# Shifted copies of a state-space kernel matrix: by matmul, or through DRAM

## The chip, the core and the metric

The kernel runs on one core of one Trainium2 chip. The metric is the device time of one execution in microseconds (us); lower is better. The engines are named as in the profile: PE is TensorE (its matmuls; PEld is its loading of weights), DVE is VectorE, ACT is ScalarE, POOL is GpSimd, SP is the engine that issues most of the DMAs. Each engine works through its own list of instructions in order.

## The reference, cut to what matters

The model has two layers on a sequence of 256 tokens and 2048 channels. The first layer mixes tokens with a diagonal state-space model (S5), 128 groups of 16 channels with a complex state of 64 each, and then a gated linear unit (GLU) of 2048 x 4096. The second is an attention layer. Each is followed by a convolutional gated feed-forward layer.

```python
def step(carry, ub):
    h_re, h_im = carry
    x_re = jnp.einsum('blgp,gnp->blgn', ub, bb_re)
    x_im = jnp.einsum('blgp,gnp->blgn', ub, bb_im)
    ...
    acc_re, acc_im, hl_re, hl_im = lax.associative_scan(combine, (a_r, a_i, x_re, x_im), axis=1)
    hs_re = acc_re * h_re[:, None] - acc_im * h_im[:, None] + hl_re
    hs_im = acc_re * h_im[:, None] + acc_im * h_re[:, None] + hl_im
    y = (jnp.einsum('blgn,gpn->blgp', hs_re, c_re) - jnp.einsum('blgn,gpn->blgp', hs_im, c_im)
         + d_skip * ub)
    return (hs_re[:, -1], hs_im[:, -1]), y
...
y = jax.nn.gelu(y)
val, gate = jnp.split(y @ w_glu.astype(f32) + b_glu.astype(f32), 2, axis=-1)
return (val * jax.nn.sigmoid(gate)).astype(dtype)
```

Such a state-space model is linear, so its output is also a sum over earlier tokens of a small kernel matrix per group and per distance in time, times the input.

## The kernel before

The sequence is cut into 32 chunks of 8 tokens. Within a chunk the output is the input times a 128x128 block Toeplitz matrix per group (8 tokens x 16 channels on both sides): the block that leads from token s to token t depends on t - s alone. Between chunks a state is carried, by a scan on DVE.

The stage `s5` handles the 128 groups in 16 steps of 8 groups, each 2 columns `g` (NG) by 4 rows `j` of groups. For one step n:

- `lead` / `part_a` builds, on DVE, `f1`, `f2` and `e1` (the powers of the state's decay with C and B multiplied in) from loads `bc` and `g4`. `powers` runs every fourth step, `frames` (sines and cosines) every second.
- `part_k` turns the input to `U` and computes with 16 small matmuls the kernel matrix `K`: 32 rows for each `j`, of which the upper 16 are used, and for each `g` 240 columns, 128 of kernel values and 112 of zeros. Then the Toeplitz matrix `TP` is made from it: its row block s is the row block of `K` shifted by 16 s columns. ACT evicts `K` from PSUM, and DVE adds the skip term to it (L452).
- `part_e` transposes `e1` to `ET`. `part_v` gives the chunk's contribution to the state `vs`, `part_r` turns and scans it to `R`, `part_h` gives the states `H` before each chunk.
- `part_c` adds the local part (`U` with `TP`) and the carried part (`H` with `f1`, `f2`) to the output `py`, which goes through a GELU to `yg`. `part_d` transposes four steps' worth of `yg` to the GLU's input.
- After every fourth step four units of early GLU work come free (`glu_early`, 24 matmuls of 128x512 on a 1 MB piece of weights each); one is taken per step.

The loop is software-pipelined: iteration n does `part_v` and `part_r` of step n-1, `part_c` of step n-2, `part_k` and `part_e` of step n, and `lead` of step n+1. A scheduling layer then fixes the order on each engine; the code's order and its dependencies are its input, and it may take instructions of neighbouring steps past each other.

`T` makes a buffer: `K` has 2 (`Ks`), `TP` 2, `U` 3. PSUM has 8 banks, 4 under the name `wk` and 4 under `acc`. The early GLU units use two `acc` banks each.

All small matmuls go through `tiled`, which uses a quarter of PE's columns at a time: 32 columns, with `tile_position` going through 0, 32, 64, 96 in turn.

Of the kernel before, what the change touches and what calls it, by code (L numbers as in the profile page):

```python
# [8 lines left out]
F32 = mybir.dt.float32  # L9
F32R = mybir.dt.float32r  # L10
I32 = mybir.dt.int32
AF = mybir.ActivationFunctionType
# [3 lines left out]
P = 128  # L16
# [21 lines left out]
HOLD = ((0, 2), (4, 6), (8, None), (None, None))  # L38

C_ID, C_PS, C_PR, C_BO, C_DM, C_MK, C_CV = 0, 128, 256, 384, 512, 528, 592  # L40
C_SG, C_NSG, C_TPI, C_FR, C_RS, C_HP, C_MH, C_END = 624, 625, 626, 627, 628, 629, 630, 638


@with_exitstack
def tile_trunk(ctx: ExitStack, tc: tile.TileContext, a: dict):
    nc = tc.nc
    act, dve, pool, pe, sync = nc.scalar, nc.vector, nc.gpsimd, nc.tensor, nc.sync
    cnt = [0]

    def T(pl, shape, dt=F32, tag=None, bufs=None):  # L50
        cnt[0] += 1
        kw = {"bufs": bufs} if bufs else {}
        return pl.tile(shape, dt, tag=tag, name=f"{tag}_{cnt[0]}", **kw)
# [8 lines left out]
    def wk():  # L62
        return T(ps, [P, 512], F32, "wk")
# [4 lines left out]
    cst = T(cp, [P, C_END], F32, "cst")  # L68
# [190 lines left out]


    def s5(f):
        with tc.tile_pool(name="s5", bufs=2) as q1, tc.tile_pool(name="s5d", bufs=4, space=bass.MemoryType.DRAM) as dp:
            w0 = env["wp"]
            dt = T(q1, [P, P], F32, "dt", 1)
            sync.dma_start(dt, a["sL"].partition_broadcast(P))
# [28 lines left out]
            r, nn = T(q1, [P, P], F32, "R"), T(q1, [P, P], F32, "w2")  # L294
# [94 lines left out]
            NG = 2  # L389
# [4 lines left out]
            def tiled(*terms):  # L394
                o = wk()[:, : NG * P]
                for g in range(NG):
                    for i, (lhs, rhs) in enumerate(terms):
                        for j in range(4):
                            pe.matmul(  # L399
                                o[32 * j : 32 * j + 32, g * P : (g + 1) * P], lhs(g, j), rhs(g, j),  # L400
                                start=g == 0 and i == 0, stop=g == NG - 1 and i == len(terms) - 1,
                                tile_position=(0, 32 * j),
                            )
                return o

            def by_group(z):
                return z.rearrange("p (g t) -> p g t", g=NG)

            def flat2(z):
                return z.rearrange("p s q -> p (s q)")  # L410
# [27 lines left out]
            def part_k(sb, e1, ff):  # L438
                puv = wk()[:, : NG * P].rearrange("p (g t) -> p g t", g=NG)
                for g in range(NG):  # L440
                    gi = NG * sb % 8 + g
                    pe.transpose(puv[:, g, :], Xn[sb // PB][:, gi, :], ident)
                U = T(q1, [P, NG, P], F32, "U", 3)
                act.activation(U, puv, AF.Copy)

                def e67(g, j):
                    return flat2(e1[:, 4 * g + j, 6:8, :])

                pkg = by_group(tiled(*((e67, lambda g, j, z=z: flat2(z[:, 4 * g + j, 1:9, :])) for z in ff)))
                K = Ks[sb % 2]  # L450
                act.activation(K[:, :, :112], pkg[:, :, :112], AF.Copy)
                dve.tensor_tensor(  # L452
                    K[:, :, 112:128],
                    pkg[:, :, 112:128],
                    dB.rearrange("p (g q) -> p g q", q=16)[:, NG * sb : NG * (sb + 1), :],
                    op=ALU.add,
                )
                RW = 4 * NG * 240
                kd = T(dp, [32, RW], F32, "kd")
                act.dma_start(kd.rearrange("r (j w) -> j r w", j=4), K.rearrange("p g c -> p (g c)"))  # L460
                TP = T(q1, [P, 4, NG, 240], F32, "TP")
                TPf = TP.rearrange("p j g c -> p (j g c)")[:, : RW - 112]
                act.dma_start(TPf, bass.AP(kd.tensor, kd.offset + 16 * RW, [[16, 8], [RW, 16], [1, RW - 112]]))
                return U, TP

            def part_e(e1):
# [47 lines left out]

            def part_c(sb, yg, ff, U, TP, H):
                def h(g, j):
                    return H[:, 4 * g + j, :]

                py = tiled(
                    (lambda g, j: U[:, g, 32 * j : 32 * j + 32], lambda g, j: TP[:, j, g, :P]),  # L520
                    *((h, lambda g, j, z=z: flat2(z[:, 4 * g + j, 0:8, :])) for z in ff),
                )
                o = (sb % PB) * 16 * NG
                act.activation(
                    yg[:, :, o : o + 16 * NG].rearrange("p t (g q) -> p g t q", q=16),
                    py.rearrange("p (g t q) -> p g t q", g=NG, q=16),
                    AF.Gelu_apprx_tanh,
                )
# [19 lines left out]

            todo, ab, fr, U, TP, ET, H = [], {}, {}, {}, {}, {}, {}
            nb = 4 * PB  # L550
# [16 lines left out]
            for n in range(nb + 2):  # L567
                if 0 <= n - 1 < nb:
                    vs = part_v(U[n - 1], ET.pop(n - 1))
                if n >= 2:  # L570
                    m = n - 2
                    if m % PB == 0:
                        yg = T(q1, [P, 8, P], F32, "yg", 1)
                    part_c(m, yg, ab.pop(m)[1], U.pop(m), TP.pop(m), H.pop(m))
                if 0 <= n - 1 < nb:
                    R = part_r(n - 1, vs, *fr[n - 1])
                if n < nb:
                    U[n], TP[n] = part_k(n, *ab[n])
                    ET[n] = part_e(ab[n][0])
                if 0 <= n - 1 < nb:  # L580
                    H[n - 1] = part_h(n - 1, R, *fr.pop(n - 1))
                if n >= 2 and m % PB == PB - 1:
                    part_d(m // PB, yg)
                    todo.append(glu_steps(m // PB))
                lead(n + 1)
                if n < 3:
                    scale_x(rs, n + 1)
                if todo and next(todo[0], True) is True:
                    todo.pop(0)
# [453 lines left out]
    ng = a["norm_g"]  # L1043
    f = f_pair()
    todo = s5(f)
    env["ap"] = ctx.enter_context(tc.tile_pool(name="ap", bufs=1))
    env["xp"] = ctx.enter_context(tc.tile_pool(name="xp", bufs=1))
# [28 lines left out]
def _constants():  # L1076
    import numpy as np

    c = np.zeros((P, C_END), np.float32)
    p = np.arange(P)  # L1080
    c[p, C_ID + p] = 1.0
    c[p, C_PS + (p + 64) % P] = 1.0
    c[p, C_PR + (p ^ 32)] = 1.0
    c[:, C_BO : C_BO + P] = (p[:, None] % 32) == (p[None, :] % 32)
    c[:, C_DM : C_DM + 16] = (p[:, None] % 32 - 16) == np.arange(16)[None, :]
    c[:64, C_MK : C_MK + 64] = -1e30
    c[:, C_CV : C_CV + 32] = np.arange(32)
    sg = np.where(p < 64, -1.0, 1.0)
    c[:, C_SG] = sg
    c[:, C_NSG] = -sg  # L1090
    c[:, C_TPI] = -sg * TWO_PI
    fr = np.float32(10000.0) ** (-np.arange(0, 64, 2, dtype=np.float32) / np.float32(64))
    c[:, C_FR] = fr[p % 32]
    c[:, C_RS] = np.where(p % 64 < 32, -1.0, 1.0)
    c[:, C_HP] = math.pi / 2
    c[:, C_MH : C_MH + 8] = -0.5
    return c


def _arrays(i):  # L1100
# [8 lines left out]
    def blocks(re, im):  # L1109
# [4 lines left out]
    pn = lambda v: v.reshape(KT, P).T  # L1114
    arrays = {
        "cst": _constants(),
        "x": g("x")[0],
        "xs": g("x")[0].reshape(32, 8, 4, 512).transpose(1, 2, 0, 3).reshape(8, P, 512),
# [46 lines left out]
```

## Time and profile before

| what | value |
|---|---|
| median of 3 runs | 2263.45 us (2258.99 to 2265.07) |
| the profiled execution | 2263.12 us, span 2261.3 us |
| busy, share of the span: PE | 2087.9 us, 92% |
| DVE | 1412.9 us, 62% |
| ACT | 1095.6 us, 48% |
| POOL | 76.5 us, 3% |
| DMA, mean over the span | 174 GB/s |

The busy shares are means over stages of different kinds. The 16 steps of the state-space model lie between 20 and 312 us; the rest of the GLU, the feed-forward layers and the attention layer follow, with PE busy nearly all of the time. The profile's rows are read so: a line of the kernel, the engine, the operation, the buffer written and those read, then how many, and how long. An entry such as `[8.14 <-DMA TP<-kd]` says that the engine was idle for 8.14 us before the row, and that the transfer into `TP` ended that. PEclk is the clock that PE was granted, as a share of full speed. A line of a helper such as `tiled` (L399) stands for many uses; the names tell them apart (`wk<-TP,U`, `wk<-f,H`, `wk<-f,e`, `wk<-ET,U`).

### The profile page before, as it was taken

Reading aid. Unit: us, or ns where it says so; the run is one execution under the profiler, and the core shown is the slowest. Engines: PE = TensorE matmul, PEld = TensorE weight load, DVE = VectorE, ACT = ScalarE, POOL = GpSimd, SP = SyncE. Lnnn points to the kernel's source line nnn. Section 1 sums busy time; section 2 is a strip of 40 time slices with the busy share of each in tenths; the row PEclk is TensorE's granted clock in tenths of the full one; section 3 lists DMA queues with packets and bytes.
Section 4 is the critical chain, followed back from the end, with each engine's and each line's share of the span. In section 5 each row is a group of like instructions: output and inputs, shape, how many; then the busy total and the mean of one; then the engine's idle time right before and its main releaser. Section 6 shows DMA issues by size and latency. Waiting matters only on the chain. (4 is left out here: it accounts for less than half of the span.)

```text
span 2261.3 us, 30415 instructions
## 1 busy us (share of the span) xinstructions
PE 2087.9 (92%) x12244; PEld 1769.7 (78%) x12244; DVE 1412.9 (62%) x1904; ACT 1095.6 (48%) x1655; POOL 76.5 (3%) x93
## 2 busy tenths in 40 slices
PE   2576789899999999999998999989999999999997
PEld 1455567688888888888886899878888888888886
DVE  6777756666546655665667666476645655665566
ACT  5454434445545544553454455545545543554444
POOL 0000001200000000000002000120000000000001
PEclk9788899999999999999999999999999999999999
DMA  4455577646555555555555433545555555565554
GB/s 147 108 130 120 131 210 220 184 152 199 184 194 187 186 186 192 188 180 194 193 191 166 135 117 122 189 166 164 185 186 192 186 186 190 190 197 185 189 186 149
DMA packets 285245, 393.28 MB, mean 174 GB/s; under 512 B 9392, under 2 KB 198448, under 8 KB 284080
## 3 DMA queue, kind: packets, MB, share of 16 engines
q1 hardware_dynamic: 280816, 372.60, 50.8%
q10 hardware_dynamic: 4288, 18.74, 3.6%
q8 instruction: 96, 1.57, 0.3%
q14 instruction: 45, 0.37, 0.1%
HBM read 385.29 MB, written 6.03 MB: 173 GB/s over the span
## 5 line engine op out<-in xcount | busy, mean ns | idle before, releaser
L74 DVE TENSOR_TENSOR wlo<-raw,whi 128x1024 fp32r<-128x1024 f32 (+2 forms) x640 | 763.8, 1196 | 590.2 <-ACT whi L73 586.9
L73 ACT ACTIVATE whi<-raw 128x1024 fp32r<-128x1024 f32 (+2 forms) x640 | 658.0, 1031 | 646.5 <-PE wk L114 233.8
L114 PE MATMUL wk<-act,whi 128*128 128x512 f32 x2688 | 944.9, 396 | 0.0
L115 PE MATMUL wk<-act,wlo 128*128 128x256 f32 x2688 | 754.4, 281 | 0.0
L114 PEld LDWEIGHTS wk<-act,whi 128*128 128x128 f32 x2688 | 504.3, 188 | 121.0
L115 PEld LDWEIGHTS wk<-act,wlo 128*128 128x128 f32 x2688 | 507.9, 189 | 0.3
L109 PE MATMUL acc<-wlo,hh 128*128 128x512 f32 x652 | 255.8, 392 | 0.5
L108 PE MATMUL acc<-whi,hh 128*128 128x512 f32 x652 | 255.5, 392 | 0.0
L110 PE MATMUL acc<-whi,hl 128*128 128x512 f32 x652 | 254.4, 392 | 0.0
L109 PEld LDWEIGHTS acc<-wlo,hh 128*128 128x128 f32 x652 | 122.5, 188 | 28.5 <-DVE wlo L74 2.2
L108 PEld LDWEIGHTS acc<-whi,hh 128*128 128x128 f32 x652 | 122.5, 188 | 27.3 <-ACT hh L73 0.5
L110 PEld LDWEIGHTS acc<-whi,hl 128*128 128x128 f32 x652 | 122.5, 188 | 26.9
L109 PE MATMUL acc<-wlo,act 128*128 128x512 f32 (+1 forms) x332 | 129.6, 392 | 4.3 <-DVE wlo L74 4.2
L108 PE MATMUL acc<-whi,act 128*128 128x512 f32 (+1 forms) x332 | 130.0, 395 | 0.8 <-ACT act L73 0.4
L110 PE MATMUL acc<-whi,act 128*128 128x512 f32 (+1 forms) x332 | 127.3, 385 | 0.0
L166 POOL TENSOR_TENSOR f<-f,gb 128x512 f32<-128x512 f32 x24 | 38.1, 1593 | 1901.5 <-issue 1586.3
L109 PEld LDWEIGHTS acc<-wlo,act 128*128 128x128 f32 x332 | 65.0, 196 | 20.1 <-DVE wlo L74 8.2
L755 DVE SCALAR_TENSOR_TENSOR cv<-gs,cw,cv 128x255 f32<-128x255 f32 (+1 forms) x168 | 77.1, 480 | 3.0
L108 PEld LDWEIGHTS acc<-whi,act 128*128 128x128 f32 x332 | 64.7, 197 | 14.9 <-ACT whi L73 1.7
L110 PEld LDWEIGHTS acc<-whi,act 128*128 128x128 f32 x332 | 64.5, 194 | 11.3 <-issue 0.2
L753 ACT ACTIVATE cv<-gs,cb,cw 128x256 f32<-128x256 f32 x84 | 50.4, 601 | 36.7 <-DVE gs L705 36.7
L399 PE MATMUL wk<-TP,U 128*32 128x128 f32 x256 | 20.5, 369 | 47.4 <-DMA TP<-kd 42.5
(281 smaller groups left out, 2377.7 us busy)
## 6 DMA issues: line engine op xcount, KB each, us to landing
raw<-in_w_gate SPq DMA_DIRECT2D x88, 1024.0 KB
raw<-in_w_up SPq DMA_DIRECT2D x88, 1024.0 KB
raw<-in_w_down SPq DMA_DIRECT2D x88, 1024.0 KB
raw<-in_w_glu SPq DMA_DIRECT2D x32, 1024.0 KB
raw<-in_w_o SPq DMA_DIRECT2D x16, 1024.0 KB
TP<-kd ACTq DMA_DIRECT2D x16, 904.0 KB
raw<-in_w_ukv SPq DMA_DIRECT2D x8, 1024.0 KB
gb<-in_norm_g SPq DMA_DIRECT2D x6, 1024.0 KB
```

The costliest lines, as they stand in the source:

```text
L73: act.activation(hi, src, AF.Copy)
L74: (eng or dve).tensor_tensor(lo, src, hi.bitcast(F32), op=ALU.subtract)
L108: pe.matmul(o, lh, rh, start=first, stop=False)
L109: pe.matmul(o, lh, rl, start=False, stop=False)
L110: pe.matmul(o, ll, rh, start=False, stop=last)
L114: pe.matmul(ov, lh, r, start=first, stop=False)
L115: pe.matmul(ov[:, 0, :], ll, r[:, 0, :], start=False, stop=last)
L166: (dve if n == NCH - 1 else pool).tensor_tensor(c, c, g[0][:, n * 512 : (n + 1) * 512], op=ALU.mult)
L399: pe.matmul(o[32 * j : 32 * j + 32, g * P : (g + 1) * P], lhs(g, j), rhs(g, j), start=g == 0 and i == 0, stop=g == NG - 1 and i == len(ter ...
L753: act.activation(cv[:, ft, :], gv[:, ft, :], AF.Identity, scale=cw[:, 2, n : n + 1], bias=cb[:, n : n + 1])
L755: dve.scalar_tensor_tensor(cv[:, ft, sh:], gv[:, ft, : S - sh], cw[:, 2 - sh, n : n + 1], cv[:, ft, sh:], op0=ALU.mult, op1=ALU.add,)
```

## The change

Before, `part_k` wrote `K` to a DRAM buffer `kd` with one DMA, laid out as 32 rows, and read it back with a second DMA whose address pattern starts each of 8 row blocks 16 columns further on. Both DMAs were issued from ACT's queue, and the second waits for the first.

After, `TP` is made by matmuls. For each `j` and each shift, a 128x32 selection matrix of zeros and ones (a slice of the constant table, which grows from 638 to 894 columns) picks the 16 rows of `K` that belong to `j` and puts them into 16 of 32 output rows, while the moving operand is `K` from column r on, 128 columns for each of the two `g`. An even and an odd shift share 32 output rows and are added up in PSUM. That makes 2 x 2 x 2 x 4 = 32 matmuls a step into two `acc` banks, and ACT evicts each bank with one copy of 128x512. `TP` loses the zero padding: 128 instead of 240 columns per group.

```diff
-C_SG, C_NSG, C_TPI, C_FR, C_RS, C_HP, C_MH, C_END = 624, 625, 626, 627, 628, 629, 630, 638
+C_SG, C_NSG, C_TPI, C_FR, C_RS, C_HP, C_MH, C_SL, C_END = 624, 625, 626, 627, 628, 629, 630, 638, 894
...
-                RW = 4 * NG * 240
-                kd = T(dp, [32, RW], F32, "kd")
-                act.dma_start(kd.rearrange("r (j w) -> j r w", j=4), K.rearrange("p g c -> p (g c)"))
-                TP = T(q1, [P, 4, NG, 240], F32, "TP")
-                TPf = TP.rearrange("p j g c -> p (j g c)")[:, : RW - 112]
-                act.dma_start(TPf, bass.AP(kd.tensor, kd.offset + 16 * RW, [[16, 8], [RW, 16], [1, RW - 112]]))
+                TP = T(q1, [P, 4, NG * P], F32, "TP")
+                for jj in range(2):
+                    bank = accb()
+                    for j in range(2):
+                        for odd in range(2):
+                            o = C_SL + (2 * (2 * jj + j) + odd) * 32
+                            for b in range(4):
+                                r = 16 * (2 * b + odd)
+                                pe.matmul(
+                                    bank[32 * b : 32 * b + 32, j * 256 : (j + 1) * 256].rearrange("p (g c) -> p g c", g=NG),
+                                    cst[:, o : o + 32], K[:, :, r : r + P],
+                                    start=j == 0 and odd == 0, stop=j == 1 and odd == 1, tile_position=(0, 32 * b),
+                                )
+                    act.activation(TP[:, 2 * jj : 2 * jj + 2, :], bank.rearrange("p (j c) -> p j c", j=2), AF.Copy)
                 return U, TP
...
-                    (lambda g, j: U[:, g, 32 * j : 32 * j + 32], lambda g, j: TP[:, j, g, :P]),
+                    (lambda g, j: U[:, g, 32 * j : 32 * j + 32], lambda g, j: TP[:, j, g * P : (g + 1) * P]),
...
+    for j in range(4):
+        for odd in range(2):
+            q = np.arange(16)
+            c[32 * j + 16 + q, C_SL + (2 * j + odd) * 32 + 16 * odd + q] = 1.0
```

The lines behind the change are 8 higher than before (L503 becomes L511), and the new matmuls are L466, the new evictions L471. What this does to the order is shown at two places. The first is PE's list in the step n = 2, before the change: the transposes of `e`, the matmul on `R` of the step before, then `ET,U` (for `vs`) mixed with the first matmuls on `TP` of the step before.

```order
L471 MATMUL wk_519<-cst_73,e_108_417 128x128 x4
L471 MATMUL wk_525<-cst_73,e_108_417 128x128 x4
L503 MATMUL wk_531<-R_488,cst_73 128x256
L399 MATMUL wk_563<-ET_518,U_493 32x128 x4
L399 MATMUL wk_575<-TP_383,U_360 32x128
L399 MATMUL wk_563<-ET_518,U_493 32x128 x4
L399 MATMUL wk_575<-TP_383,U_360 32x128 x3
```

The same place on PE after the change:

```order
L479 MATMUL wk_616<-cst_73,e_110_481 128x128 x4
L479 MATMUL wk_622<-cst_73,e_110_481 128x128 x4
L466 MATMUL acc_579<-K_43_178,cst_73 32x256 x16
L466 MATMUL acc_597<-K_43_178,cst_73 32x256 x16
L511 MATMUL wk_628<-R_552,cst_73 128x256
L399 MATMUL wk_660<-ET_615,U_557 32x128 x8
L399 MATMUL wk_672<-TP_412,U_391 32x128 x4
```

The 32 new matmuls stand between the transposes of `e` and the matmul on `R`, and need `K` of the same step; everything behind them is in the old order.

The second place is ACT's list one step earlier, before the change: the eviction of `K`, those of `ET`, the store of `K`, `vs`, other work, and then the load of `TP`, ahead of the next output (L524).

```order
L451 ACTIVATE K_44_181<-wk_362 128x2x112
L472 ACTIVATE ET_385<-wk_386 128x512
L472 ACTIVATE ET_385<-wk_392 128x512
L460 DMA kd_381<-K_44_181 4x32x480
L478 ACTIVATE vs_447<-wk_438 128x2x128
L479 ACTIVATE vs_447<-wk_438 128x2x64
L420 ACTIVATE bc_538<-bc_538,cst_73 128x128
L421 ACTIVATE bc_538<-bc_538 128x128
L494 ACTIVATE dc_45_184<-mag_18_114 128x8x31
L73 ACTIVATE whi_975<-raw_969 128x1024
L463 DMA TP_383<-kd_381 128x1x1808
L524 ACT_TABLE_LOAD
```

And after it:

```order
L451 ACTIVATE K_44_179<-wk_393 128x2x112
L480 ACTIVATE ET_449<-wk_450 128x512
L480 ACTIVATE ET_449<-wk_456 128x512
L420 ACTIVATE bc_815<-bc_815,cst_73 128x128
L502 ACTIVATE dc_45_182<-mag_18_112 128x8x31
L419 ACTIVATE bc_635<-bc_635,cst_73 128x128
L421 ACTIVATE bc_815<-bc_815 128x128
L471 ACTIVATE TP_412<-acc_413 128x512
L471 ACTIVATE TP_412<-acc_431 128x512
L486 ACTIVATE vs_511<-wk_502 128x2x128
L487 ACTIVATE vs_511<-wk_502 128x2x64
```

The two DMAs are gone, and two evictions of `TP` stand ahead of the two of `vs`.

More of the change, by code (lines that the diff above doesn't have):

```diff
@@ L261, in s5 @@
     def s5(f):
-        with tc.tile_pool(name="s5", bufs=2) as q1, tc.tile_pool(name="s5d", bufs=4, space=bass.MemoryType.DRAM) as dp:
+        with tc.tile_pool(name="s5", bufs=2) as q1:
             w0 = env["wp"]
```

## Prediction

> **What bounds the kernel now.** I read the busy time by stretch first, then the waits in the stretch that the change touches, then the instructions in order of time. The end of the program is set by TensorE (PE), and from 312 us on the order of its instructions is the same in both programs but for a few neighbours. So the question is how long the state-space stage lasts, from 20 us to 312 us. Columns after the stretch: busy us of PE, PEld, DVE, ACT, POOL with instruction counts, then the granted PE clock, the DMA share and GB/s.
>
> ```profile
> 54.90:119.80 64.90, 41.60 (x556) 32.11 (x557) 48.91 (x85) 26.85 (x64) 0.18 (x2) 0.73 0.43 107
> ...
> 20.00:312.00 292.00, 188.93 (x2058) 142.90 (x2062) 210.24 (x339) 130.12 (x282) 1.35 (x6) 0.81 0.52 127
> ```
>
> PE works 189 of 292 us, at a granted clock of 0.81; DVE works 210. No engine is full, so the stage is a chain with holes. These are the holes between 20 and 320 us (us in total, times, longest):
>
> ```profile
> PE wk L399 <- DMA TP<-kd: 42.5, 12, 8.6
> PE wk L399 <- ACT ET L472: 15.2, 6, 7.1
> ...
> ACT vs L478 <- PE wk L399: 23.3, 8, 7.4
> ACT vs L478 <- DMA kd<-K: 22.6, 4, 9.3
> ACT bc L420 <- DMA bc<-in_sBC: 22.2, 4, 9.8
> ...
> ACT act L73 <- DMA kd<-K: 12.7, 3, 5.5
> ACT L524 <- DMA kd<-K: 9.6, 1, 9.6
> ...
> DVE w L490 <- PE wk L488: 39.3, 8, 9.0
> ```
>
> PE stands 42.5 us before the matmuls that need `TP`. ACT stands another 44.9 us (22.6, 12.7 and 9.6) before the issue of the load, because its queue is in order and the load waits for the store. DVE's largest hole, 39.3 us, is PE's hole passed on. One round trip shows why:
>
> ```profile
> 44.89 0.55 ACTq L460 DMA_DIRECT2D kd<-K  x1
> 57.60 0.61 ACTq L463 DMA_DIRECT2D TP<-kd  x1
> 70.05 0.39 PE L399 MATMUL wk<-TP,U 128*32 128x128 f32 x1 [8.14 <-DMA TP<-kd]
> ```
>
> The store is issued at 44.9, the load can be issued at 57.6, the matmul starts at 70.1: 25 us for one step, two in flight.
>
> **Removed.** (1) The PE waits for `TP`: -42.5. DVE was idle 81.8 us of the 292, more than all that is removed, so I take the whole; if DVE is late next, half of it. (2) ACT's stand before the load. PE felt it where `vs` was queued behind it:
>
> ```profile
> 132.57 0.47 PE L487 MATMUL wk<-cst,vs 128*128 128x128 f32 x1 [4.77 <-ACT vs L478]
> 151.03 0.47 PE L487 MATMUL wk<-cst,vs 128*128 128x128 f32 x1 [3.11 <-ACT vs L478]
> 299.34 0.47 PE L487 MATMUL wk<-cst,vs 128*128 128x128 f32 x1 [3.89 <-ACT vs L478]
> ```
>
> Together -11.8. The rest of ACT's 44.9 lies beside PE's own waits and is not counted again.
>
> **Added on PE.** Each of the 16 steps gets 32 fp32 matmuls, 32 columns wide, 256 elements moving, four column groups in turn. The nearest rows are the same form with 128 moving, at a low and at a full clock (each fp32 matmul is two records, so x8 is four matmuls):
>
> ```profile
> 85.39 0.68 PE L399 MATMUL wk<-TP,U 128*32 128x128 f32 x8
> 85.81 1.11 PE L399 MATMUL wk<-f,H 128*32 128x128 f32 x16
> ...
> 126.97 0.40 PE L399 MATMUL wk<-TP,U 128*32 128x128 f32 x8
> 127.19 0.62 PE L399 MATMUL wk<-f,H 128*32 128x128 f32 x16
> ```
>
> Start to start, four matmuls take 0.42 us slow and 0.22 us fast: 105 and 55 ns each. With 256 elements 210 and 110 ns, so 32 take 6.72 or 3.52 us a step, and 16 steps 107.5 or 56.3 us. That is the largest term, and its size hangs on the clock. Cheaper than 56.3 it can't be, since the fast row is already at full clock.
>
> The clock moves the old work too. In a step 24 matmuls stand on `TP` and `H` (24 x 50 ns = 1.2 us between slow and fast), six transposes of `vs` and `U`, and 16 matmuls on `f` and `e`:
>
> ```profile
> 87.12 0.42 PE L488 MATMUL wk<-cst,vs 128*128 128x128 f32 x1
> 87.33 0.42 PE L487 MATMUL wk<-cst,vs 128*128 128x128 f32 x1
> 88.33 1.68 PE L399 MATMUL wk<-f,e 128*32 128x128 f32 x32
> ...
> 116.97 1.08 PE L399 MATMUL wk<-f,e 128*32 128x128 f32 x32
> 117.98 0.77 PE L471 MATMUL wk<-cst,e 128*128 128x128 f32 x5
> ...
> 140.12 0.27 PE L488 MATMUL wk<-cst,vs 128*128 128x128 f32 x1
> 140.22 0.27 PE L487 MATMUL wk<-cst,vs 128*128 128x128 f32 x1
> ```
>
> A transpose is 0.21 or 0.10 us (six: 0.64), the `f,e` group 1.68 or 1.08 us (0.60). Together 2.44 us a step, 39 us in the stage, to be had at most. Call h the share of work at half speed (granted clock = 1 - h/2). New work less what the old work gains is then 56.3 + 51.2 h - 39 (1 - h) = 17.3 + 90 h us, between 17.3 and 107.3. Where PE has few holes the clock is this:
>
> ```profile
> 300.00:320.00 20.00, 18.60 (x118) 14.61 (x117) 12.96 (x20) 7.62 (x10) 0.00 (x0) 0.88 0.57 166
> 380.00:400.00 20.00, 20.00 (x90) 16.27 (x88) 11.75 (x13) 9.45 (x10) 0.00 (x0) 1.00 0.70 200
> ```
>
> 0.88 and 1.00, near 0.95, so h = 0.1: +26.3. I take it because the 8 us holes go and 3.5 us of solid work come in.
>
> **New waits.** PE now needs `K` itself, right behind the transposes of `e`. Before, only a DMA waited for it, so the trace has the time at which it was ready: the end of DVE's L452, against PE's next matmul there (L503), which would now be the first of the 32.
>
> ```profile
> 77.22 0.60 PE L503 MATMUL wk<-R,cst 128*128 128x256 f32 x2
> 77.08 0.18 DVE L452 TENSOR_TENSOR K<-wk,dB 128x32 f32<-128x32 f32 x1
> 91.35 0.70 PE L503 MATMUL wk<-R,cst 128*128 128x256 f32 x2 [0.32 <-DVE R L498]
> 92.82 0.19 DVE L452 TENSOR_TENSOR K<-wk,dB 128x32 f32<-128x32 f32 x1 [0.28 <-ACT K L451]
> 104.67 0.61 PE L503 MATMUL wk<-R,cst 128*128 128x256 f32 x2
> 105.63 0.18 DVE L452 TENSOR_TENSOR K<-wk,dB 128x32 f32<-128x32 f32 x1
> 255.41 0.60 PE L503 MATMUL wk<-R,cst 128*128 128x256 f32 x2
> 255.57 0.18 DVE L452 TENSOR_TENSOR K<-wk,dB 128x32 f32<-128x32 f32 x1
> ```
>
> `K` came 0.04, 1.66, 1.14 and 0.34 us late, 0.80 in the mean: 16 x 0.80 = +12.7, ends 0 and 26.6 (always 1.66). Behind it wait the `R` matmul, the next step's `vs` and DVE's scan.
>
> ACT gets 32 evictions of 128x512. The same form is this:
>
> ```profile
> L472 ACT ACTIVATE ET<-wk 128x512 f32<-128x512 f32 x32 | 18.1, 594 | 4.1 <-PE wk L471 2.0 <-DVE w L505 1.0 <-DVE w L506 0.4
> ```
>
> 32 x 0.594 = 19.0 us. ACT works 130 of 292, and nobody needs `TP` for a step; but the second eviction stands ahead of `vs` in ACT's queue. PE meanwhile does the `R` and `ET,U` matmuls, some 0.35 us at full clock, so about 0.25 us shows: +4, ends 0 and 19.0.
>
> PE changes between full and column-group matmuls twice more a step. After the fast `f,e` group (16 x 55 ns = 0.88) the next row begins 1.01 us later: 0.13 us a change, 32 changes, +4.2; ends 0 and, at the 0.18 us by which a fast group outlasts its next start, 5.8.
>
> **DMA.** Between 40 and 320 us these two queues move nearly all (MB, share of the 16 engines' time), and ACT's, q10, has nothing but these stores and loads:
>
> ```profile
> q10 hardware_dynamic: 4284, 18.74, 28.8%
> q1 hardware_dynamic: 9611, 16.94, 23.6%
> ```
>
> Without q10 the `bc` and weight loads land sooner. PE felt those through `ET` (15.2 us); half of it, -7, ends -15.2 and 0. The ACT queue loses 32 issues; SP's queue changes order a little and loses none. The constant table grows by 128 x 256 x 4 = 131 KB; at 127 GB/s +1.0 ahead of the inputs.
>
> **The sum.** -42.5 - 11.8 + 26.3 + 12.7 + 4.0 + 4.2 - 7.0 + 1.0 = -13.1. The profiled execution took 2263.12 us, 0.3 under the median of the runs, so 2250.0.
>
> **The rivals.** *All covered:* PE stays at full clock (h = 0), `K` is ready in time and the evictions are hidden. For it: 16 steps without a hole over 2 us. Against: DVE would then work 210 of some 253 us, in order. -54.3 + 17.3 + 4.2 - 7 + 1 = -38.8, 2224. With h = 0 alone and the rest as summed, 17.3 stands for 26.3, and the time is 2241; it belongs to this case, a quarter of its chance. The Trainium skill's page TensorE: Matmul & The Clock Gate, section "Why this matters for your kernels", asks only that no idle gap exceeds about 3 us, which would make h = 0 wherever such holes go. The trace agrees from 380 to 400 us (1.00), and not from 300 to 320 us (0.88).
>
> *The evictions show:* all 19.0 us of ACT's new work end up on the path, behind the second bank and ahead of `vs`, and 2250 + 15 = 2265: no change. For it: ACT's waits on PE for `vs` (23.3 us) show that this edge is tight. Against: the first of the two banks is free while PE works on the second. The Trainium skill's page TensorEngine Tiling (Array Packing), section "Performance Considerations", warns of just this: tiling speeds up the matmuls and not the emptying of PSUM, which may become the bottleneck. No run so far shows it here.
>
> *PE turns the bound at half clock:* the 32 matmuls stand behind the wait for `K`; if that hole and the wait for `vs` keep the clock at 0.75 (h = 0.5; the first steps had 0.73), 17.3 + 45 takes the place of 26.3: +36, 2286, slower. It decides from h = 0.25, a granted clock of 0.88, on. Against: those steps had 8 us holes.
>
> **How the numbers follow.** My forecast 0.42, all covered 0.16, no change (evictions, or h near 0.25) 0.22, half clock 0.20. A measurement of this kernel tells about 0.3% (6.8 us) from no change, so faster 0.58, same 0.22, slower 0.20. The range reaches from 2222, just under the rival with all covered, to 2284, just short of half clock.
>
> **What would show it.** No wait on `TP`; the 32 matmuls at 3.5 to 4 us a step; granted clock in the stage near 0.95; PE's waits on `K` near 13 us; ACT's 32 new evictions near 0.6 us; `bc` waits shorter; the last `TP` matmul some 13 us earlier. Wrong it is if the clock stays at 0.8, if the 32 matmuls don't run four abreast, or if DVE takes over the holes.

## The result and the profile after

The changed kernel took 2209.59 us (median of four runs, 2207.51 to 2211.37), the kernel before in the same session 2262.15 us. The ratio is 0.9759, 95% interval 0.9731 to 0.9786: 2.4% faster, some 54 us where 13 were forecast, and below the forecast range. The profiled execution has a span of 2207.7 us.

From the second half of the GLU on, the two profiles differ by a nearly constant shift. A landmark there is line 191 (PE), whose first and last starts stand behind the durations (ns, least, median, most). First before, then after:

```profile
L191 PE MATMUL acc<-xh,f x128: 270/275/552, 456.2 to 1521.6; 128*128 128x128 f32 x128
```

```profile
L191 PE MATMUL acc<-xh,f x128: 270/275/553, 405.3 to 1468.3; 128*128 128x128 f32 x128
```

50.9 us are won ahead of that line's first start, and 53.3 by its last. The stretches that were shown of before now read so (same columns):

```profile
20.00:312.00 292.00, 255.16 (x3265) 185.56 (x3266) 248.86 (x381) 182.68 (x354) 7.80 (x11) 0.98 0.35 107
...
20.00:263.00 243.00, 210.73 (x3064) 151.14 (x3068) 210.70 (x337) 158.87 (x322) 1.32 (x6) 0.98 0.25 73
...
54.90:119.80 64.90, 56.80 (x911) 39.09 (x901) 63.74 (x109) 40.82 (x89) 0.40 (x5) 0.97 0.21 60
```

The granted clock rose from 0.81 to 0.98, the DMA share fell from 0.52 to 0.35. The stage now ends at 263 us, and up to there PE and DVE both work 211 of 243 us; from 54.9 to 119.8 us DVE is busy 63.7 of 64.9. The stage is no longer a chain with holes: in that stretch DVE is nearly full, and PE not far from it. The waits between 20 and 320 us:

```profile
PE wk L495 <- ACT vs L486: 7.7, 5, 4.2
...
PE acc L466 <- DVE K L452: 4.7, 7, 1.1
...
ACT whi L73 <- DMA raw<-in_w_glu: 14.4, 6, 3.8
ACT TP L471 <- PE acc L466: 10.9, 12, 1.6
ACT bc L420 <- DMA bc<-in_sBC: 8.0, 7, 1.9
...
DVE w L498 <- PE wk L496: 4.3, 3, 2.2
```

PE waits neither for `TP` nor for `ET` any more. The wait that was put in, PE for `K`, is 4.7 us in all. ACT's waits for `bc` fell from 22.2 to 8.0, DVE's hole of 39.3 to 4.3. The new matmuls, in order of time on PE:

```profile
58.67 1.09 PE L479 MATMUL wk<-cst,e 128*128 128x128 f32 x8
60.17 3.66 PE L466 MATMUL acc<-K,cst 128*32 128x256 f32 x64 [0.41 <-DVE K L452]
63.77 0.70 PE L511 MATMUL wk<-R,cst 128*128 128x256 f32 x2
```

32 of them (64 records) take 3.60 us from start to start, 112 ns each; 16 steps make 57.6 us. The last of the rows answering to those before are ACT's evictions and, from the DMA table between 40 and 320 us, the only queue left besides instruction fetch:

```profile
L471 ACT ACTIVATE TP<-acc x32: 573/582/599, 41.9 to 247.2; 128x512 f32<-128x512 f32 x32
```

```profile
q1 hardware_dynamic: 15024, 29.60, 34.8%
```

### The profile page after: what moved, and what is told of

It reads as the page before. It is cut to its first block, busy times and chain, and to the rows that moved or that the text cites. A ratio compares the mean times of both kernels' runs of the same rounds, so it can differ in the third digit from the quotient of the medians.

```text
span 2207.7 us, 32426 instructions
## 1 busy us (share of the span) xinstructions
PE 2109.7 (96%) x13268; PEld 1779.4 (81%) x13268; DVE 1415.1 (64%) x1904; ACT 1125.0 (51%) x1695; POOL 75.7 (3%) x93
## 5 line engine op out<-in xcount | busy, mean ns | idle before, releaser
L108 PE MATMUL acc<-whi,hh 128*128 128x512 f32 x652 | 255.6, 392 | 0.0
L108 PEld LDWEIGHTS acc<-whi,hh 128*128 128x128 f32 x652 | 122.5, 188 | 27.4 <-ACT hh L73 0.5
L108 PE MATMUL acc<-whi,act 128*128 128x512 f32 (+1 forms) x332 | 126.4, 381 | 0.9 <-ACT act L73 0.7
L109 PE MATMUL acc<-wlo,act 128*128 128x512 f32 (+1 forms) x332 | 124.8, 377 | 2.3 <-DVE wlo L74 2.3
L110 PE MATMUL acc<-whi,act 128*128 128x512 f32 (+1 forms) x332 | 124.2, 375 | 0.0
L166 POOL TENSOR_TENSOR f<-f,gb 128x512 f32<-128x512 f32 x24 | 37.3, 1555 | 1866.7 <-issue 1583.9
L108 PEld LDWEIGHTS acc<-whi,act 128*128 128x128 f32 x332 | 62.5, 188 | 12.7 <-ACT act L73 1.0
L466 PE MATMUL acc<-K,cst 128*32 128x256 f32 x1024 | 60.3, 388 | 5.0 <-DVE K L452 4.7
```

Of the source, the lines that this page charges most:

```text
L108: pe.matmul(o, lh, rh, start=first, stop=False)
L109: pe.matmul(o, lh, rl, start=False, stop=False)
L110: pe.matmul(o, ll, rh, start=False, stop=last)
L166: (dve if n == NCH - 1 else pool).tensor_tensor(c, c, g[0][:, n * 512 : (n + 1) * 512], op=ALU.mult)
L466: pe.matmul(bank[32 * b : 32 * b + 32, j * 256 : (j + 1) * 256].rearrange("p (g c) -> p g c", g=NG), cst[:, o : o + 32], K[:, :, r : r + P ...
```

## The experiments

The question is why 54 us came and not 13. Each kernel ran beside the kernel before on the same chip, so kernels are compared by their ratio to it; one hundredth of a ratio is 22.6 us. The scheduler orders some instructions of e1, e2, e4 and e7 otherwise than in the kernel that they start from; what that is worth was not measured.

| kernel | median us | ratio to before, 95% interval |
|---|---|---|
| after | 2209.6 | 0.9759 (0.9731 to 0.9786) |
| e1 before, DMAs issued by POOL | 2247.9 | 0.9931 (0.9910 to 0.9952) |
| e2 before, with the new matmuls unread | 2248.1 | 0.9939 (0.9920 to 0.9957) |
| e3 after, with store and load unread | 2248.3 | 0.9940 (0.9921 to 0.9960) |
| e4 after, new matmuls twice | 2258.2 | 0.9988 (0.9976 to 0.9999) |
| e5 after, ungated load unread | 2301.0 | 1.0167 (1.0138 to 1.0196) |
| e6 as e3, four `bc` | 2238.8 | 0.9892 (0.9867 to 0.9917) |
| e7 before, four `bc` | 2259.0 | 0.9987 (0.9970 to 1.0003) |
| e8 after, four `bc` | 2205.8 | 0.9745 (0.9721 to 0.9770) |
| e9 after, constant `TP` | 2188.4 | 0.9693 (0.9676 to 0.9709) |
| e10 as e9, with store and load unread | 2239.8 | 0.9908 (0.9876 to 0.9939) |
| e11 after, with the store unread | 2233.0 | 0.9887 (0.9873 to 0.9902) |
| e12 as e8, `f2` on POOL | 2237.5 | 0.9910 (0.9896 to 0.9925) |
| e13 as e11, four `bc` | 2212.0 | 0.9765 (0.9744 to 0.9786) |
| e14 after, gated load unread | 2247.3 | 0.9918 (0.9889 to 0.9948) |
| e15 as e8, skip term on PE | 2205.4 | 0.9743 (0.9720 to 0.9766) |
| e16 after, landing tile for `bc` | 2208.6 | 0.9751 (0.9724 to 0.9778) |
| e17 as e16, with store and load unread | 2219.2 | 0.9797 (0.9769 to 0.9825) |
| e18 as e16, skip term on PE | 2210.2 | 0.9758 (0.9733 to 0.9784) |

### The parts of the change: e1 to e4

e1 is the kernel before with its two DMAs issued from POOL's queue, so that ACT no longer stands before the load:

```diff
-                act.dma_start(kd.rearrange("r (j w) -> j r w", j=4), K.rearrange("p g c -> p (g c)"))
+                pool.dma_start(kd.rearrange("r (j w) -> j r w", j=4), K.rearrange("p g c -> p (g c)"))
...
-                act.dma_start(TPf, bass.AP(kd.tensor, kd.offset + 16 * RW, [[16, 8], [RW, 16], [1, RW - 112]]))
+                pool.dma_start(TPf, bass.AP(kd.tensor, kd.offset + 16 * RW, [[16, 8], [RW, 16], [1, RW - 112]]))
```

> The kernel before, with its store of K and its load of TP issued from POOL's queue, so that ACT never stands before the load; the round trip itself stays. Theory (the length of the round trip holds PE): PE still waits 30 us or more for TP, the time falls by no more than 12 us, about 2250 to 2262. Rival (ACT's standing in line was the cost): ACT's waits on the store were 50 us in all, and with them gone at least half of the gain of the change appears, 2235 or less.

It won 15.6 us (0.0069), which lies between the two ranges and nearer the theory. PE's wait for the round trip stayed as it was (PE's waits, 20 to 312 us):

```profile
PE wk L399 <- DMA TP<-kd: 40.8, 11, 10.6
```

So ACT's stand before the load seems to have a price of its own, near the 11.8 of the forecast, and it isn't the missing 40 us.

e2 is the kernel before with the 32 selecting matmuls put in behind the load; nobody reads their result, and they aren't evicted:

```diff
+                for jj in range(2):
+                    bank = accb()
+                    ...
+                                pe.matmul(
...
```

> The kernel before with the 32 selecting matmuls of each step added, their banks left unread, while TP still comes through DRAM. Theory (the wait decides, a warm clock alone buys nothing): some 57 us of new PE work, part of it in the holes; PE still waits 25 us or more for TP, granted clock up from 0.81 to 0.88 or more, time 2260 to 2290. Rival (the gain is PE's clock, and the matmuls bring it by filling the holes): clock near 1.0 and the time 2245 or less.

With 57 us more work on PE the kernel before became 13.8 us faster, not slower, so the theory is out; the rival's 2245 us and a clock near 1.0 were not quite reached either. PE's waits in e2:

```profile
PE wk L499 <- ACT vs L490: 28.6, 9, 5.2
...
PE wk L399 <- DMA TP<-kd: 3.8, 3, 2.3
```

The matmuls went into the holes before `TP` (42.5 us before, 3.8 now), and the granted clock of the stage rose from 0.81 to 0.93, with which the old work grew shorter (PE was busy for 20.5 us with the matmuls on `TP` before, and for 13.8 in e2). What PE waits for instead is ACT's `vs`. So with the wait for `TP` nearly gone and the new matmuls done, only 13.8 of the 54 us are there.

e3 is the kernel after with the removed store and load put back into a tile that nobody reads:

```diff
+                RW = 4 * NG * 240
+                kd = T(dp, [32, RW], F32, "kd")
+                pool.dma_start(kd.rearrange("r (j w) -> j r w", j=4), K.rearrange("p g c -> p (g c)"))
+                TQ = T(q1, [P, 4, NG, 240], F32, "TQ", 1)
+                TQf = TQ.rearrange("p j g c -> p (j g c)")[:, : RW - 112]
+                pool.dma_start(TQf, bass.AP(kd.tensor, kd.offset + 16 * RW, [[16, 8], [RW, 16], [1, RW - 112]]))
```

> The changed kernel with the store and the load still done, into a buffer that nobody reads, from POOL's queue, so that only the traffic of 18.7 MB comes back. Theory (PE's waits behind late bc and weight loads came from that traffic, some 16 us): 2217 to 2230, ACT's waits on bc and on weights up by 10 us or more. Rival (traffic costs nothing, all of the gain is the wait for TP): 2207 to 2213.

It lost 40.9 of the 54.5 us (0.0181), far more than the theory's range allows. All other instructions of PE, DVE, ACT and SP are the same in the same order, so this is the price of 16 stores and 16 loads that no other work needs. The waits of ACT, DVE and PE show who pays:

```profile
ACT bc L420 <- DMA bc<-in_sBC: 36.9, 9, 8.4
...
DVE bc L418 <- DMA bc<-in_sBC: 31.6, 7, 7.9
...
PE wk L501 <- ACT vs L492: 29.4, 7, 8.9
```

And one load of `bc`, from SP's issue to ACT's first use of it, first in the kernel after:

```profile
62.06 0.33 SPq L415 DMA_DIRECT2D bc<-in_sBC  x1
...
64.67 0.40 ACT L420 ACTIVATE bc<-bc,cst 128x128 f32<-128x128 f32 x1 [0.17 <-DMA bc<-in_sBC]
```

and then the same load in e3:

```profile
59.61 0.33 SPq L415 DMA_DIRECT2D bc<-in_sBC  x1
...
70.48 0.40 ACT L420 ACTIVATE bc<-bc,cst 128x128 f32<-128x128 f32 x1 [8.43 <-DMA bc<-in_sBC]
71.28 0.36 ACT L492 ACTIVATE vs<-wk 128x256 f32<-128x256 f32 x1
```

2.6 us after the issue in the one, 10.9 us in the other, and `vs`, for which PE waits, stands right behind it in ACT's queue. Over the loads of `bc` from 20 to 312 us the time from issue to landing (least, median, most) is, after and in e3:

```profile
DMA to landing us min/median/max: 2.5/2.6/6.8
```

```profile
DMA to landing us min/median/max: 2.5/6.6/10.8
```

One thing differs from the kernel before: e3 sends the traffic out from POOL's queue (q0, 7424 packets between 20 and 312 us), the kernel before from ACT's (q10, 4288). e2 still has it on ACT's, and there too `bc` lands late:

```profile
DMA to landing us min/median/max: 6.5/7.3/11.8
```

e2 stands 40.7 us (0.0180) above the kernel after, as e3 does. But ACT's waits for the store (16.0 and 8.7 us), PE's 3.8 us for `TP` and another order are in that difference as well, so the price of the traffic on ACT's queue alone is not measured.

e4 makes every selecting matmul of the kernel after twice:

```diff
-                    for j in range(2):
+                    for rj in range(4):
+                        j = rj % 2
```

> The changed kernel with every selecting matmul done twice, 64 a step, the second set starting the sums anew. Theory (PE is now the fuller engine, with 32 us of holes left in the stage, half of which can't be filled): 57 us more PE work, time up by 30 to 55 us, 2240 to 2265. Rival (DVE sets the pace, with 211 of 243 us, and PE's work lies beside it): up by less than 20 us, under 2230.

The second dose cost 51.8 us (0.0229) for its 57.6 us of work: it finds hardly any holes. Stage and DVE's longest wait in e4:

```profile
20.00:312.00 292.00, 264.52 (x4111) 183.79 (x4112) 215.73 (x339) 151.89 (x315) 1.30 (x6) 1.00 0.21 61
```

```profile
DVE w L515 <- PE wk L512: 31.5, 13, 7.6
```

PE at 264.5 of 292 us and at full clock is then the bound. The kernel after stands just short of that.

### Traffic and matmuls apart: e9 and e10

In e9 the matmuls and evictions of the kernel after are replaced by one constant tile; e10 adds the unread store and load of e3.

```diff
-                TP = T(q1, [P, 4, NG * P], F32, "TP")
-                for jj in range(2):
-                    ...
+                if "TPc" not in env:
+                    env["TPc"] = T(q1, [P, 4, NG * P], F32, "TPc", 1)
+                    pool.memset(env["TPc"], 0.0)
+                TP = env["TPc"]
```

> The kernel after without the selecting matmuls and their evictions; TP is one constant tile, so the shift is left out, and there is neither matmul nor DRAM traffic nor a wait for TP. It prices the first dose of the 57.7 us of selecting matmuls, as e4 priced the second (+48.6 us). If PE bounds the stage of the kernel after already: 2155 to 2175 us. If VectorE, busy 39 of 40 us there between 60 and 140 us, stands ready as the next bound: 2180 to 2200 us, with VectorE busy over 92% of the stage and the first matmuls nearly free. If the matmuls were wholly covered: 2203 to 2210 us.

> As e9, with the store and load of K put back from POOL's queue into a tile that nobody reads: traffic without the matmuls and without the wait for TP. Contention theory: the loads of bc land in 6 to 7 us in place of 2.6, and ACT and VectorE stand behind them as in e3, whether or not there are matmuls: 2225 to 2248 us, close to e3's 2248 and 35 us or more above e9. Rival (in e3 the traffic only slowed PE's own work, the matmuls and the transfers together): within 15 us of e9.

| ratio to before | no matmuls | matmuls | matmuls cost |
|---|---|---|---|
| no traffic | e9 0.9693 | after 0.9759 | 0.0066, 14.9 us |
| traffic | e10 0.9908 | e3 0.9940 | 0.0032, 7.2 us |
| traffic costs | 0.0215, 48.6 us | 0.0181, 40.9 us | |

Both came as the contention theory, and DVE as the next bound, had it. The traffic costs 41 to 49 us whether or not PE makes the shift, and the matmuls 7 to 15 us of their 57.6. The middle of the stage shows why; the stretch 60 to 200 us in e9, after and e3:

```profile
60.00:200.00 140.00, 107.86 (x1316) 79.77 (x1308) 134.94 (x222) 83.19 (x170) 0.22 (x3) 0.94 0.28 76
```

```profile
60.00:200.00 140.00, 126.58 (x1878) 90.32 (x1879) 130.36 (x209) 97.11 (x190) 0.40 (x5) 0.99 0.25 70
```

```profile
60.00:200.00 140.00, 109.10 (x1551) 77.51 (x1544) 108.29 (x175) 78.89 (x157) 10.59 (x18) 0.90 0.58 130
```

Without matmuls DVE is busy 134.9 of 140 us: DVE is nearly the floor, and most of the work of PE's matmuls lies beside it. In e9 PE waits for DVE:

```profile
PE wk L399 <- DVE e L435: 32.5, 9, 7.7
```

After, DVE works 130.4 and PE 126.6 of 140. With the traffic neither reaches 110. (The scheduler orders some instructions of e9 and e10 otherwise than those of after and e3; each pair that gives the price of traffic has one order.)

### Which transfer, and through which wait: e5, e11, e14, e6, e7, e8, e13

e5 was to give the load without the store: `K` is stored once, and the load repeated in every step. Against e3:

```diff
-                kd = T(dp, [32, RW], F32, "kd")
-                pool.dma_start(kd.rearrange("r (j w) -> j r w", j=4), K.rearrange("p g c -> p (g c)"))
+                if "kd" not in env:
+                    env["kd"] = T(dp, [32, RW], F32, "kd", 1)
+                    pool.dma_start(env["kd"].rearrange("r (j w) -> j r w", j=4), K.rearrange("p g c -> p (g c)"))
+                kd = env["kd"]
```

> The kernel after, with the load of 128 x 1808 words from DRAM put back in every step from POOL's queue into a tile that nobody reads; the store of K is made once, in the first step, so that after it no transfer hangs on K and K's buffer is held by none. Contention theory (the bytes of the round trip hold up the other queue's loads of bc, ACT and VectorE stand, PE stands behind them): the load has about 926 KB of the 1,170 KB of store and load, so most of the 39 us that store and load together cost the kernel after comes back: 2232 to 2250 us, ACT's waits for bc 25 us or more in 20 to 312 us. Rival (the 39 us came from the wait of the store for K, from K's buffer held by the store, or from the order): 2208 to 2220 us, waits for bc near the 8 us of the kernel after.

2301 us, outside both ranges and inconclusive. Held by no store, each load followed as soon as the one before had landed, and two small fills of `z` stood behind them in POOL's queue, for which DVE waited:

```profile
DVE pu L370 <- POOL z L358: 70.8, 1, 70.8
```

e14 mends that with a store of 16 columns (8 KB) ahead of each load, which ties it to its step; e11 has the store and no load.

```diff
+                pool.dma_start(kd.rearrange("r (j w) -> j r w", j=4)[:, :, 112:128], K[:, 0, 112:128])
```

> The kernel after with, in each step from POOL's queue, a store of 16 columns of K (8 KB) and behind it the whole load of 904 KB, read by nobody: the load's bytes at nearly e3's moments, without the store's. If the bytes set the price: 2232 to 2245 us. If the store, being issued just ahead of the loads of bc, has most of e3's 39 us, and the load falls between them: 2212 to 2228 us. POOL's two small fills of z stand behind these transfers in its queue, so up to 20 us could come from there; VectorE's waits for z would show it.

> The kernel after with the store of K alone (240 KB a step from POOL's queue), read by nobody. If the bytes set the price, a fifth of the 39 us of e3 at most: 2210 to 2222 us, loads of bc landing in about 3 us. If the store's wait for K, its hold on K's buffer or the issue from POOL's queue set it: 2230 to 2250 us.

The load, with its small store, costs 36.0 us over the kernel after (0.0159), and DVE does not wait for the fills of `z` there; the store alone, with a fifth of the bytes, 29.0 (0.0128); together they cost 40.9. So the bytes don't set the price, and for the store the theory that they do falls. In e11 the median landing of `bc` grows by 1.1 us only, to 3.7, yet ACT stands 20 us longer:

```profile
ACT bc L420 <- DMA bc<-in_sBC: 28.4, 8, 5.7
```

In most steps of e11 the store of `K` is issued within two us of a load of `bc`, in some before it and in some behind. The rows of the same load show one before it:

```profile
60.48 0.69 POOL L474 DMA_DIRECT2D kd<-K  x1 [10.58 <-DVE K L452]
...
62.01 0.33 SPq L415 DMA_DIRECT2D bc<-in_sBC  x1
...
68.42 0.40 ACT L420 ACTIVATE bc<-bc,cst 128x128 f32<-128x128 f32 x1 [3.96 <-DMA bc<-in_sBC]
```

Issued 1.5 us behind the store, the load is used 6.4 us later, where it took 2.6 in the kernel after. e13 takes the coincidence away with four buffers for `bc`; e8, e7 and e6 have the same edit in the kernel after, in the kernel before and in e3:

```diff
-                bc4 = T(q1, [P, 4, NP, 16], F32, "bc")
+                bc4 = T(q1, [P, 4, NP, 16], F32, "bc", 4)
```

> e11 (the kernel after with the store of K beside it, 2233 us) with four buffers for bc. If the store costs its 23 us only because it is issued within two us of a load of bc that ACT soon waits for, then loads issued one or two steps ahead hide the longer landing: 2205 to 2217 us, ACT's waits for bc under 10 us (28.4 in e11). If the store's bytes or its hold on K's buffer slow the stage in another way: 2225 to 2236 us.

> The kernel after with four buffers for bc. ACT still waited 8 us for bc there (7 waits). If these are on the path: 2200 to 2207 us. If PE, which is busy 211 of 243 us there, covers them: 2207 to 2213 us. A changed order of the loads could also cost some us.

> The kernel before with four buffers for bc in place of two and nothing else. If late loads of bc were a loss of their own in the kernel before, beside the waits for TP: ACT's 22 us of waits for bc shrink to under 10, PE's 15 us for ET shrink too, and the time is 2238 to 2252 us. Rival (PE's waits for TP take up whatever is gained, since TP is what comes last there): 2255 to 2266 us.

> The kernel after with store and load beside it, as in e3, and four buffers in place of two for the tile bc, so that SP issues the loads of bc up to two steps earlier. Contention theory: the transfers are as long as in e3, but they now land ahead of their use: ACT's waits for bc fall from 36.9 us to under 12, VectorE's from 31.6 to under 10, and the time falls from 2248 to 2212 to 2228 us. Rival (bc is only named, the loss sits in the order of the issues or in TensorE's clock): 2238 to 2255 us, whatever the waits for bc do.

In e13 the store cost 4.5 us over e8 (0.0020) where it had cost 29.0, as that theory of the coincidence has it, though ACT's wait stayed above the 10 us that I expected:

```profile
ACT bc L420 <- DMA bc<-in_sBC: 12.6, 5, 4.9
```

e7 won nothing that can be told from no change. ACT's waits for `bc` fell from 22.2 to 9.5 us, and PE's holes stayed nearly as they were:

```profile
PE wk L399 <- DMA TP<-kd: 39.0, 10, 7.5
PE wk L487 <- ACT vs L478: 15.5, 7, 5.5
PE wk L399 <- ACT ET L472: 15.1, 6, 6.0
```

So in the kernel before, earlier `bc` alone buys nothing that shows while those holes are there. e6 won only 10.9 us of 40.9 (0.0048), against my expectation, and beside e8, which has the same order without the traffic, the round trip still costs 33.2 us (0.0147): the four buffers let the scheduler place ACT's use of `bc` earlier too, and ACT again waited right behind the issue (30.7 us in all).

### The whole price through `bc`: e16 and e17

Here loads go into a tile of their own with three buffers, and the scalings write from it into `bc`, which keeps two. The order on PE, DVE and ACT is the same in both kernels; e17 has the store and load of e3 beside it.

```diff
-                bc4 = T(q1, [P, 4, NP, 16], F32, "bc")
-                sync.dma_start(bc4, a["sBC"][sb])
+                bcr = T(q1, [P, 4, NP, 16], F32, "bcr", 3)
+                sync.dma_start(bcr, a["sBC"][sb])
...
-                act.activation(bc4[:, 2], bc4[:, 2], AF.Copy, scale=cst[:, C_NSG : C_NSG + 1])
+                act.activation(bc4[:, 2], bcr[:, 2], AF.Copy, scale=cst[:, C_NSG : C_NSG + 1])
...
```

> The kernel after with a landing tile of three buffers for the loads of bc, and the scalings written from it into bc (two buffers as before), so that a load can be issued as soon as the scalings of an earlier step are done. ACT's 8 us of waits for bc go: 2200 to 2208 us, as e8. If PE covers them: 2207 to 2213 us.

> e16 with store and load of K beside it from POOL's queue, as in e3, in the same order of all other instructions. If the round trip's price goes through late loads of bc alone: within 10 us of e16, 2203 to 2216 us, waits for bc under 10 us. If the weights' loads, the issue from POOL's queue or the clock carry a part: that part stays, 2218 to 2240 us.

The same traffic now costs 10.4 us (0.0046), where it cost 40.9; 2219 us lies at the low end of the second range: most of the price went through `bc`, and a part stays. The loads still land late, but nobody waits for them; e17's landing times and its stage up to 263 us (the profiled run is e17's fastest, 2213.6 us):

```profile
DMA to landing us min/median/max: 2.6/5.7/11.8
```

```profile
20.00:263.00 243.00, 210.44 (x3080) 150.72 (x3080) 210.74 (x338) 159.81 (x323) 22.39 (x38) 0.99 0.64 147
```

With a DMA share of 0.64 PE and DVE work as much in this stretch as in e16 without the traffic (211.9 and 210.5 us). So about three quarters of the price of the traffic went through late `bc` (a rough share, since e17's runs spread over 9.7 us). Of the rest, the weights' loads may be one part, which no run separates: ACT's wait for them in e17, and in e16:

```profile
ACT whi L73 <- DMA raw<-in_w_glu: 21.0, 9, 8.7
```

```profile
ACT whi L73 <- DMA raw<-in_w_glu: 12.9, 7, 3.8
```

### Versions: e12, e15, e18

Three kernels went on from e8 and e16: `f2` computed on POOL, and the skip term of `K` added by four small matmuls in PSUM so that ACT alone evicts `K`.

```diff
-                dve.tensor_tensor(f2, zt(1, 0, 9, 1), bc(3, 9), op=ALU.mult)
+                pool.tensor_tensor(f2, zt(1, 0, 9, 1), bc(3, 9), op=ALU.mult)
```

```diff
-                act.activation(K[:, :, :112], pkg[:, :, :112], AF.Copy)
-                dve.tensor_tensor(
-                    K[:, :, 112:128],
-                    ...
+                act.activation(K[:, :, :P], pkg, AF.Copy)
```

> The kernel after with four buffers for bc (2205.8 us in e8) and the product f2 computed on POOL in place of VectorE, 16 products of 128 x 1152. If VectorE's work is on the path of the stage: 2190 to 2203 us. If PE covers it: 2203 to 2208 us. If POOL is slow enough that f2 comes late: 2208 to 2225 us.

> e8 (the kernel after with four buffers for bc, 2205.8 us) with the skip term of K added by four small matmuls in PSUM in place of VectorE's addition of 128 x 32, so that ACT alone evicts K and the selecting matmuls wait for no VectorE. PE waited 4.6 us for VectorE's part of K in e8 and VectorE gives up 16 additions of 0.18 us; PE takes on 64 matmuls of 32 x 32 at 0.05 to 0.1 us. If VectorE's place in the chain to K counted: 2198 to 2205 us. If not: 2204 to 2212 us.

> e16 with the skip term of K added by four small matmuls in PSUM, as in e15: the version with neither wait. 2197 to 2206 us if the two add up; 2203 to 2212 us if PE, busy 215 of 243 us in e15, bounds both.

e12 lost 37.3 us against e8 (0.0165). The same product, on POOL in e12 and on DVE in the kernel after:

```profile
L431 POOL TENSOR_TENSOR f<-z,bc 128x1152 f32<-128x1152 f32 x16 | 51.3, 3214 | 185.2 <-PE wk L399 105.1 <-ACT vs L487 55.9 <-DVE bc L418 9.8
```

```profile
L431 DVE TENSOR_TENSOR f<-z,bc 128x1152 f32<-128x1152 f32 x16 | 21.6, 1347 | 0.0
```

3.2 us against 1.35, and PE then waited 16.2 us for `K`, which hangs on `f2`. e15 equals e8, and e18 equals e16: the wait for `K` is worth nothing that these runs can tell. Of the kernels that make the shift, e8 and e15 have the lowest medians (2205.8 and 2205.4 us), but their intervals overlap that of the kernel after; a version that is surely faster was not found. PE and DVE at 87% of the stage each leave little.

## Why the prediction was wrong

The direction was right; the forecast was 41 us short, and one step made it so.

**DMA: "half of it, -7, ends -15.2 and 0".** This is the step that failed. Taking the traffic away gave -40.9 us (e3 against the kernel after; on POOL's queue, as said above), 34 us beyond the term and far beyond its end. I had taken the price of late `bc` and weight loads from one of PE's waits, the 15.2 us for `ET`. But ACT's 22.2 us for `bc` stood in the same view, `vs` stands behind it in ACT's queue, and e7 shows that while `TP` comes last earlier `bc` buys nothing: such a price can't be read off PE's rows until that wait is gone. That the price shows only then is argued from e7 and e3; no run takes the traffic alone from the kernel before. The rows of before that bounded it were DVE's work: 210 of 292 us. After the change DVE does that work within 243 us, and the time that DVE idled before (81.8 us) was the end that the range needed. The Trainium skill's page DMA: Bandwidth & Descriptors, section "Issuing engines are not separate DMA queues", says that transfers issued by different engines run on the same 16 DMA engines and interleave; the landing times of SP's `bc` (a median of 2.6 us without POOL's transfers, 6.6 beside them) agree with it. I had looked at the queues' shares and not used them so.

**The exchange of the wait for matmuls.** -42.5 - 11.8 + 26.3 + 12.7 + 4.0 + 4.2 = -7.1 with the traffic left in place. e3 is that kernel: -13.6 us (-17.9 to -9.0). This part of the sum was off by some 6 us. That it came so near is partly luck: in e3 PE waits 30.2 us for `vs` (15.0 before), where the sum takes 11.8 off, and no more for `ET` (15.2 before), which the sum leaves. Its terms one by one:

- The wait for `TP` went whole, as taken. DVE did not take it over while the traffic ran (108.3 of 140 us in e3); it does so without the traffic.
- ACT's stand: PE's waits for `vs` fell from 15.0 to 8.5 us in the kernel after, not by 11.8.
- The matmuls: 3.60 us a step, against 3.52 forecast at full clock. The granted clock was 0.92 in e3's stage (h = 0.16) and 0.98 in the kernel after (h = 0.04), so h = 0.1 lies between: 31.7 for the first and 17.3 + 90 x 0.04 = 20.9 for the second, in place of 26.3. PE's busy time in the stage grew by 21.8 us (188.9 to 210.7), so the term came out; but its formula takes all old small matmuls as slow before, though a clock of 0.81 is h = 0.38, and it leaves out those of the early GLU, which got faster too (L108: 469 ns before, 413 after). That the two nearly cancel is luck.
- PE for `K`: 4.7 us, 6.0 in e3, not 12.7. The lateness read off the old order did not carry over. In two steps before it was larger than in any of the four rows shown (`K` ready at 165.9 us against 160.4, and at 242.3 against 234.9, the latter behind a wait of ACT of 9.8 us for `bc`), and after the change PE never waited more than 1.1 us. e15 shows that what remains is covered.
- The evictions: 32 x 0.582 = 18.6 us as forecast, and mostly covered: ACT waits 10.9 us for the matmuls to evict, and e9 prices matmuls and evictions together at 14.9 us; the evictions alone were not measured. The warning of the Trainium skill's page TensorEngine Tiling (Array Packing), section "Performance Considerations", does not show here, and the rival built on it falls.
- The changes of mode: not seen apart from 0.08 us a step between 3.52 and 3.60; no run measured them alone. The larger table: the first product with `bc` starts at 21.0 us after and at 21.1 before, so nothing is left of the 1.0 us.

**The rivals.** "All covered" had the state of the engines right (clock, `K`, evictions), and would have given 2224; it used the same -7 and was 14 us too high. The rule that it took from the Trainium skill's page TensorE: Matmul & The Clock Gate, section "Why this matters for your kernels", fits the kernel after: between 20 and 312 us three holes of PE above 3 us are left (7.7, 6.9 and 4.2) of 15 before, and the clock is 0.98. The 0.88 from 300 to 320 us before was no exception to it, as I took it to be: the clock was 0.50 up to 304.5 us, behind the hole of 3.89 us that ended at 299.34, and 1.00 from 304.7 on. But 3 us is no sharp edge here: in the kernel after, the clock was also 0.50 from 84.3 to 87.5 us, behind a hole of 1.7 us, and from 309.6 to 316.2, behind one of 1.9. "Half clock" fell: with the matmuls the stage's granted clock was 0.98 after, 0.93 in e2 and 0.92 in e3.

**What would show it.** The matmuls, the evictions, the shorter waits for `bc` and the missing wait for `TP` came as written; PE's waits on `K` were 4.7 us, not 13, and the last matmul on `TP` came 48.8 us earlier (262.9 us, 311.7 before), not 13.

## What to carry to other kernels

When a change takes transfers off a stage, price the traffic as well as the wait: list each load that lands beside them, how long before its use it is issued, and what stands behind its consumer in an in-order queue. The waits in the trace don't add up to that price while another wait comes last, so bound the gain by the work of the next busiest engine in the stage. Loads that are issued just ahead of their use were cheap here only as long as little else was in flight (2.6 us to landing, 6.6 beside the round trip); a landing tile with a buffer more takes most of that risk away, provided that the order doesn't move the use forward with it.

## What was not expected of the hardware

- A store of 240 KB that nobody waits for cost 29.0 us over 16 steps, issued (in the step shown) 1.5 us ahead of a 256 KB load of another queue; with those loads issued earlier it cost 4.5 us.
- Beside stores of 240 KB and loads of 904 KB, the latter with a median landing of 12.2 us (e3), 256 KB loads of another queue landed after 6.6 us in place of 2.6, and the 1 MB weight loads after 9.9 in place of 6.2.
- More matmuls on a PE with holes can go with a faster kernel: with 57 us of unread work the granted clock rose from 0.81 to 0.93 and the time fell by 13.8 us (e2). The order of the instructions changed too, so the share of the clock is not separated.
- The product of 128x1152 fp32 elements with broadcast operands took 3.2 us in the mean on POOL (2.3 to 5.9) against 1.35 us on DVE.
